# The raw weight blocks of block products go to Pool's DMA queue

## Chip, core and metric

The kernel runs on one core of a Trainium2 chip. The metric is device time in microseconds (us) for one execution; several executions are timed and their median is compared. The engines are named as the profile names them: PE (TensorE, matmuls), PEld (its weight loads), DVE (VectorE), ACT (ScalarE), POOL (GpSimd) and SP (SyncE, which here only issues DMAs). A name with q, such as SPq, is an engine's instruction queue.

## The reference, cut to what matters

The reference is one inference step of a two-layer decoder trunk for a prompt of 1024 tokens and 8 sample tokens that share all weights. What the change touches is the feed-forward block of each layer, with a model width of 1024 and a hidden width D_FF of 2816:

```python
def swiglu(h, w_gu, w_down):
    gate, up = jnp.split(h @ w_gu, 2, axis=-1)
    return (jax.nn.silu(gate) * up) @ w_down
```

Around it stand an HGRN2 recurrence or a stick-breaking attention, an attention into memory tokens, and RMS norms. All is float32.

## The kernel before, in words

Tokens are worked on in two groups, g = 0 (512 prompt tokens) and g = 1 (512 prompt tokens and the 8 sample tokens, 520 columns). Activations lie transposed, features on the 128 partitions. To keep float32 accuracy, every operand of a matmul is split into a high part (rounded to fp32r) and a low part (the rest), and each product is three matmuls: high by high, high by low, low by high. For a weight block this means a load of the raw float32 block, a cast on ACT (high part) and a subtraction on DVE (low part), then the matmuls. `split_w` (load at L254, cast L259, subtraction L260) does that for an ordinary block; its raw tile comes from the pool `wraw` with 5 buffers.

The hidden width is cut into 22 slices f of 128 columns, and these into five parts of 5, 5, 4, 4 and 4 slices (`PARTS`). A part computes gate and up for its slices and then adds their share of the down projection for all eight output blocks, with weights loaded by `split_w` (`w<-in_w_down` in the profile).

For most slices the gate and up products are ordinary. For group 1 some slices use **block products** instead: the two products (gate and up, each with two halves of the contracted width and two halves of the columns) are done as seven products of half size in place of eight, with sums of weight blocks and of activation blocks as operands. `ffn(1, 0, ...)`, layer 0, does so for slices 10 to 21; `ffn_w(1, ...)`, layer 1, for slices 4 to 21. That is 12 + 18 = 30 slices.

For each such slice `sums_here` loads four raw weight blocks a11, a21, a12, a22 of 128 x 512 floats (256 KB in 512 runs of 512 bytes) in the loop at L528, and hands back a function that makes the weight of product j. The sums are DVE additions at L535: product 1 needs a21 + a22 (in the profile `b<-w` or `b<-c`, the first addition of a slice), product 2 a11 + a21 + a22, product 5 a12 on top of that. Products 0, 3 and 6 take a11, a12 and a22 as they are. `gate_up_w` casts each weight on ACT (L560), subtracts on DVE (L561), runs 12 matmuls for each product (L570, 84 for a slice) and puts the seven results together on ACT and DVE (L577 to L594; the DVE steps L588 and L590 free PSUM banks into which later matmuls of the slice write).

Buffers: in layer 0 a slice's raw blocks take two tiles of the pool `cpool` (4 buffers, tile name `c`), in layer 1 two tiles of `apool` (8 buffers, four of them held by other data there; tile name `w`), and for slice 4 alone four tiles of `wraw`. So a slice's loads can start when the slice two before it has released its tiles: after the addition and the splits of a12, and after the split of a22 for product 6.

The order of the work is partly written out by hand (the `weave` and `drain` calls at the end) and otherwise set by the framework's planner: it lists the instructions of each engine and each DMA queue in an order found by a costed replay of the program, with the buffers of the pools given out in that replay. On the chip each engine and queue then runs its list strictly in order, and waits on semaphores. A different queue for a load therefore can change the listed order of other instructions too.

All direct DMAs stand in SP's queue. POOL's queue has only 32 gathers of cache pages (`page_loader`, L992, 256 KB each in 128 rows of 2 KB), which belong to the sample tokens of layer 1 and lie between the two stages with block products, apart from the first eight at the end of the first; besides, POOL builds constants in the first 14 us.

Of the kernel before, what the change touches and what calls it, by code (L numbers as in the profile page):

```python
# [23 lines left out]
def tile_decoder(  # L24
# [6 lines left out]
    nc = tc.nc  # L31
# [491 lines left out]
    def sums_here(l, f, raws, outs):  # L523
        a11, a12, a21, a22 = raws()
        for r, k0, m0 in (
            (a11, 0, f * P), (a21, 0, DFF + f * P), (a12, 512, f * P), (a22, 512, DFF + f * P),
        ):
            nc.sync.dma_start(  # L528
                r.rearrange("p (k m) -> p k m", m=P), w_gu[l][k0 : k0 + 512, m0 : m0 + P].rearrange("(k p) m -> p k m", p=P)
            )  # L530
        kept = {}

        def add(a, b):
            t = outs()
            nc.vector.tensor_add(t, a, b)  # L535
            return t

        def weight(j):
            if j == 1:
                return add(a21, a22)  # L540
            if j == 2:
                kept[3] = add(a11, a21)
                kept[2] = add(kept[3], a22)
                return kept[2]
            if j == 4:
                return kept[3]
            if j == 5:
                return add(kept[2], a12)
            return (a11, None, None, a12, None, None, a22)[j]

        return weight
# [51 lines left out]
    class ffn_w:  # L603
# [13 lines left out]
        def raws(self):  # L617
            if self.pi:
                ts = [apool.tile([P, 2, 512], F32, tag="a", name=nm("w")) for _ in range(2)]
                return [t[:, a, :] for t in ts for a in range(2)]  # L620
            return [wraw.tile([P, 512], F32, tag="w", name=nm("w")) for _ in range(4)]

        def part(self, pi):
# [4 lines left out]
            for j in range(nf):  # L628
                self.pi = pi
                if f0 + j < self.plain:  # L630
                    mt, ins = gate_up_q(l, f0 + j, self.x)
                    mids.append(mt)
                    with tc.issue_after(ins.ins):
                        for _ in range((1, 2, 1, 0)[j]):
                            next(self.sums, None)
                else:
                    mids.append(gate_up_w(
                        sums_here(l, f0 + j, self.raws, B),
                        self.ops, self.spl, lambda: [Q(i) for i in range(4)]
                    )[0])  # L640
                yield
# [33 lines left out]
    class ffn:  # L675
# [14 lines left out]
        def part(self, pi):  # L690
# [5 lines left out]
            for j in range(nf):  # L696
                if f0 + j >= self.prod:
                    mt, gate = gate_up_w(
                        sums_here(l, f0 + j, self.raws, B),
                        self.ops, lambda: wspl.tile([P, 2, 512], F32R, tag="ws", name=nm("ws")), self.quads,  # L700
                    )
                    mids.append(mt)
                    yield
                    continue
                pg = proj(g, w_gu[l], 0, ND, (f0 + j) * P, self.xt)
                sg = silu(None, pg, g)
                pu = proj(g, w_gu[l], 0, ND, DFF + (f0 + j) * P, self.xt)
                nc.vector.tensor_mul(sv(sg, g), sv(sg, g), pv(pu, g))  # L708
                mt = M(F32R)
                split_to((mt[:, 0, :n], mt[:, 1, :n]), sg[:, :n])  # L710
                mids.append(mt)
                yield
# [853 lines left out]
```

## Time and profile before

| What | us |
|---|---|
| median of 3 runs | 2492.56 (2491.49 to 2495.53) |
| the profiled execution, its own time | 2501.9 |
| its span, first to last instruction | 2500.2 |
| PE busy in the span | 2457.2 |
| DVE busy | 1669.7 |
| ACT busy | 1202.1 |
| POOL busy | 46.6 |
| packets of SP's DMA queue, as a share of 16 DMA engines | 38.1% |

The page gives busy times for each engine, forty slices of the span, the DMA queues, the chain of work that ended last, and groups of instructions by line with what ended the idle time before them. The longer views are: who waited for whom, the chain in order of time, the timeline of one stretch, and busy times by stretch. Matmuls are pipelined, so their durations overlap and a busy PE is not a PE at its peak. The stretch with block products of layer 0 runs from about 1237 to 1419 us of the span, that of layer 1 from about 2187 to 2460 us.

### The profile page before, as it was taken

The page shows a single profiled execution, that of the slowest core. Times are in us where ns is not written, and L with a number is a line of the kernel's source. Part 1 is how long each engine was busy: PE and PEld are TensorE (multiplying, and loading weights), DVE is VectorE, ACT ScalarE, POOL GpSimd, SP SyncE. Part 2 cuts the span into 40 slices and gives each one's busy share as a digit, 9 for nine tenths or more (in the row PEclk, how much of TensorE's full clock was granted, in tenths as well). Part 3 has the DMA queues.
Part 4 walks back from the last instruction along what each step waited for, and adds up shares of the span by engine and source line. Part 5 has one row for each costly group of instructions (what it writes and reads, how often), then busy time and mean ns, then how long its engine had stood idle before and what let it go on. Part 6 is the DMA issues. An engine that isn't in the chain of part 4 may idle for free.

```text
span 2500.2 us, 40342 instructions
## 1 busy us (share of the span) xinstructions
PE 2457.2 (98%) x15421; PEld 2156.9 (86%) x15421; DVE 1669.7 (67%) x2972; ACT 1202.1 (48%) x2315; POOL 46.6 (2%) x59
## 2 busy tenths in 40 slices
PE   8999999999999999999999999999999999999998
PEld 6888988877877898999999989877777798999997
DVE  5766556654766585655877785677677558676775
ACT  5446544243433454555544554555454445554444
POOL 1000000000000000000000100021000000000000
PEclk9999999999999999999999999999999999999999
DMA  5352252233643447422233445553444243343331
GB/s 185 113 164 71 72 156 81 60 110 116 179 124 99 127 133 224 127 87 68 75 100 94 147 136 188 158 162 113 135 144 118 77 127 118 110 128 101 95 92 48
DMA packets 451595, 297.88 MB, mean 119 GB/s; under 512 B 17605, under 2 KB 414482, under 8 KB 451402
## 3 DMA queue, kind: packets, MB, share of 16 engines
q1 hardware_dynamic: 448842, 286.92, 38.1%
q0 software_dynamic: 2560, 8.39, 1.1%
q8 instruction: 121, 1.98, 0.3%
q14 instruction: 72, 0.59, 0.1%
HBM read 265.44 MB, written 29.80 MB: 118 GB/s over the span
## 4 chain that ended last, share of the span: by engine, by line
PE 89%; DVE 5%; DMA 2%; ACT 2%; issue 1%; POOL 0%; SPq 0%; DVEq 0%; ACTq 0%
PE mm L273 58%; PE q L570 5%; PE q L654 5%; PE s L1188 2%; PE q L509 2%; PE mm L1056 2%; PE mm L570 2%; PE s L570 1%; PE s L911 1%; PE s L1344 1%; PE s L870 1%; DVE b L535 1%; PE mm L820 1%; PE ns L965 1%; PE mm L847 1%
## 5 line engine op out<-in xcount | busy, mean ns | idle before, releaser
L273 PE MATMUL mm<-x,ws 128*128 128x512 f32 (+1 forms) x6624 | 1193.7, 338 | 0.0
L273 PEld LDWEIGHTS mm<-x,ws 128*128 128x128 f32 x6624 | 1009.5, 188 | 152.3 <-issue 12.2
L259 ACT CAST ws<-w 128x512 fp32r<-128x512 f32 (+1 forms) x664 | 390.5, 589 | 669.3 <-PE mm L273 518.5
L260 DVE TENSOR_TENSOR ws<-w,ws 128x512 fp32r<-128x512 f32 (+1 forms) x664 | 429.0, 649 | 262.3 <-ACT ws L259 254.0
L273 PE MATMUL mm<-m,ws 128*128 128x512 f32 (+1 forms) x2112 | 395.0, 343 | 0.3
L273 PEld LDWEIGHTS mm<-m,ws 128*128 128x128 f32 x2112 | 324.6, 189 | 50.9 <-issue 3.2
L654 PE MATMUL q<-m,ws 128*128 128x260 f32 x1056 | 128.8, 283 | 0.0
L654 PEld LDWEIGHTS q<-m,ws 128*128 128x128 f32 x1056 | 127.2, 188 | 0.4 <-ACT hT L484 0.2
L570 PE MATMUL q<-y,ws 128*128 128x260 f32 x864 | 114.3, 285 | 7.2 <-DVE t L588 7.1
L570 PEld LDWEIGHTS q<-y,ws 128*128 128x128 f32 x864 | 107.7, 189 | 9.2 <-DVE t L588 9.2
L446 DVE TENSOR_TENSOR r<-r,mm 128x512 f32<-128x512 f32 (+1 forms) x96 | 66.0, 687 | 57.0 <-PE mm L273 56.4
L560 ACT CAST ws<-b 128x512 fp32r<-128x512 f32 x120 | 74.4, 621 | 57.3 <-PE q L654 15.7
L561 DVE TENSOR_TENSOR ws<-b,ws 128x512 fp32r<-128x512 f32 x120 | 82.4, 688 | 22.9 <-ACT ws L560 21.4
L290 DVE TENSOR_SCALAR t<-mm 128x512 f32<-128x512 f32 (+1 forms) x70 | 48.3, 690 | 61.7 <-PE mm L273 61.5
L570 PE MATMUL q<-x,ws 128*128 128x260 f32 x648 | 87.7, 285 | 0.0
L570 PEld LDWEIGHTS q<-x,ws 128*128 128x128 f32 x648 | 82.7, 191 | 0.0
L708 DVE TENSOR_TENSOR t<-t,mm 128x512 f32<-128x512 f32 (+1 forms) x54 | 37.2, 688 | 56.3 <-PE mm L273 56.0
L294 DVE TENSOR_TENSOR t<-t,t 128x512 f32<-128x512 f32 (+1 forms) x54 | 37.4, 692 | 54.0 <-ACT t L293 54.0
L313 DVE TENSOR_TENSOR st<-st,n 128x512 f32<-128x512 f32 (+1 forms) x98 | 67.0, 691 | 6.6 <-ACT n L312 5.0
L280 ACT CAST m<-t 128x512 fp32r<-128x512 f32 (+1 forms) x88 | 54.8, 623 | 17.0 <-DVE t L708 8.5
L281 DVE TENSOR_TENSOR m<-t,m 128x512 fp32r<-128x512 f32 (+1 forms) x88 | 60.8, 691 | 1.5 <-ACT m L280 0.7
L570 PE MATMUL mm<-a,ws 128*128 128x260 f32 x432 | 59.0, 285 | 1.7 <-DVE t L590 1.3
(362 smaller groups left out, 2974.3 us busy)
## 6 DMA issues: line engine op xcount, KB each, us to landing
w<-in_w_gu SPq DMA_DIRECT2D x304, 256.0 KB
w<-in_w_down SPq DMA_DIRECT2D x160, 256.0 KB
w<-in_w_in_a SPq DMA_DIRECT2D x80, 256.0 KB
w<-in_w_o SPq DMA_DIRECT2D x64, 256.0 KB
c<-in_w_gu SPq DMA_DIRECT2D x48, 256.0 KB
w<-in_w_mem_kv SPq DMA_DIRECT2D x32, 256.0 KB
c<-in_cache_mem_k SPq DMA_DIRECT2D x16, 512.0 KB
c<-in_cache_mem_v SPq DMA_DIRECT2D x16, 512.0 KB
```

What stands on the lines that cost most here:

```text
L259: nc.scalar.copy(ws[:, 0, :n, :], raw[:, :n, :])
L260: nc.vector.tensor_sub(ws[:, 1, :n, :], raw[:, :n, :], ws[:, 0, :n, :].bitcast(F32))
L273: nc.tensor.matmul(ps[:, a, : PW[g]], wt, xt[k][:, xi, o : o + PW[g]], start=(k == 0 and wi == 0), stop=(k == nk - 1 and wi == 2),)
L280: nc.scalar.copy(dst[0], src)
L281: nc.vector.tensor_sub(dst[1], src, dst[0].bitcast(F32))
L313: nc.vector.tensor_add(acc[:, :n], acc[:, :n], t[:, :n])
L446: nc.vector.tensor_add(dst, dst, pv(ps, g))
L509: nc.tensor.matmul(pp[a][:, :h], wt, xt[k][:, xi, a * h : (a + 1) * h], start=(k == 0 and wi == 0), stop=(k == ND - 1 and wi == 2),)
L560: nc.scalar.copy(w[:, 0, :], src)
L561: nc.vector.tensor_sub(w[:, 1, :], src, w[:, 0, :].bitcast(F32))
L570: nc.tensor.matmul(ps[:, :h], w[:, wj, k * P : (k + 1) * P], x[:, xi, :], start=(first and k == 0 and wi == 0), stop=(k == 3 and wi == 2), ...
L654: nc.tensor.matmul(pp[a][:, :h], wt, mids[k][:, xi, a * h : (a + 1) * h], start=(k == 0 and wi == 0), stop=(k == nf - 1 and wi == 2),)
```

## The change

The four loads of `sums_here` are issued from GpSimd's (Pool's) DMA queue. Everything else, the loads of `split_w` among it, stays on SP's queue. Per execution these are 30 x 4 = 120 loads of 256 KB.

```diff
@@ -525,7 +525,7 @@ def sums_here(l, f, raws, outs):
         for r, k0, m0 in (
             (a11, 0, f * P), (a21, 0, DFF + f * P), (a12, 512, f * P), (a22, 512, DFF + f * P),
         ):
-            nc.sync.dma_start(
+            nc.gpsimd.dma_start(
                 r.rearrange("p (k m) -> p k m", m=P), w_gu[l][k0 : k0 + 512, m0 : m0 + P].rearrange("(k p) m -> p k m", p=P)
             )
```

## The prediction

> **What bounds the kernel now.** First the page's busy times, then the waits by engine, then the two stretches with block products (1237 to 1419 us and 2187 to 2460 us).
>
> ```profile
> span 2500.2 us, 40342 instructions
> PE 2457.2 (98%) x15421; PEld 2156.9 (86%) x15421; DVE 1669.7 (67%) x2972; ACT 1202.1 (48%) x2315; POOL 46.6 (2%) x59
> ```
>
> PE is busy for 2457.2 of 2500.2 us, so a change of DMA queues can win little: 43 us in the whole kernel, most of it elsewhere. Busy times by stretch show what lies open where these loads are used (the first number after the stretch's length is PE's):
>
> ```profile
> 1225.00:1300.00 75.00, 72.15 (x561) 69.04 (x560) 60.53 (x114) 38.34 (x81) 0.00 (x0) 1.00 0.37 109
> 1300.00:1360.00 60.00, 58.34 (x471) 56.77 (x470) 43.47 (x75) 28.15 (x57) 0.00 (x0) 1.00 0.33 97
> 2200.00:2300.00 100.00, 96.59 (x790) 96.16 (x790) 72.95 (x137) 49.03 (x102) 0.00 (x0) 0.98 0.36 105
> 2300.00:2400.00 100.00, 96.83 (x795) 95.46 (x794) 75.29 (x138) 48.90 (x98) 0.00 (x0) 1.00 0.36 104
> ```
>
> PE's open time in these four is 2.85 + 1.66 + 3.41 + 3.17 = 11.1 us. Now the waits: of SP for the loads' buffers, of DVE for the loads, of PE for DVE (us in total, times, longest).
>
> ```profile
> SPq L528 <- DVE ws L561: 163.2, 31, 15.1
> SPq L528 <- DVE t L594: 66.4, 18, 6.5
> DVE b L535 <- DMA w<-in_w_gu: 19.0, 14, 3.6
> DVE b L535 <- DMA c<-in_w_gu: 3.5, 6, 1.5
> PE q L570 <- DVE t L588: 7.1, 6, 3.3
> PE mm L570 <- DVE t L590: 1.3, 1, 1.3
> PE mm L570 <- DVE t L588: 0.6, 1, 0.6
> ```
>
> Read downwards these are one mechanism. SP sits at L528 because DVE has not yet released the raw tiles (229.6 us), not because SP is busy. As soon as they are released the load starts, and for 20 slices DVE waits for its landing, 22.5 us in all. DVE runs in order, so L588 and L590 of the slice before stand behind the waiting addition, and PE loses 7.1 + 1.3 + 0.6 = 9.0 us in 8 places. One round of it, from the chain in order of time:
>
> ```profile
> 2226.16 0.69 DVE ws L561
> ...
> 2227.20 0.05 SPq L528
> 2227.25 0.05 issue
> 2227.30 3.46 DMA w<-in_w_gu
> ...
> 2230.85 0.69 DVE b L535
> ...
> 2235.28 0.35 DVE t L588
> 2235.62 0.04 issue
> 2235.67 21.96 PE q L570 x180
> ```
>
> The split at 2226.16 ends near 2226.85 and releases a tile; its two loads go out, the second at 2227.30, and both have landed at 2230.76. So release to second landing is 2230.76 - 2226.85 = **3.9 us** on SP's queue. DVE then has some 4.8 us of its own work up to L588, and PE waits for that. The timeline says how much of DVE's wait came through:
>
> ```profile
> 2224.51 0.42 DVE L588 TENSOR_TENSOR t<-t,q 128x260 f32<-128x260 f32 x1
> ...
> 2230.85 0.69 DVE L535 TENSOR_TENSOR b<-w 128x512 f32<-128x512 f32 x1 [0.85 <-DMA w<-in_w_gu]
> ...
> 2235.20 0.42 DVE L588 TENSOR_TENSOR t<-t,q 128x260 f32<-128x260 f32 x1
> ...
> 2235.67 1.50 PEld L570 LDWEIGHTS q<-y,ws 128*128 128x128 f32 x12 [0.33 <-DVE t L588]
> ```
>
> 0.85 us of waiting on DVE cost PE's weight load 0.33, so about 0.5 us was covered; the slice takes 2235.20 - 2224.51 = 10.7 us. The loads are just in time, and every further microsecond from release to landing meets a path with at most half a microsecond left.
>
> **The change part by part.**
>
> *Removed from SP: 120 issues.* The view of line L528 gives their lengths (ns, least, median, most):
>
> ```profile
> L528 SPq DMA_DIRECT2D w<-in_w_gu x72: 367/498/1947, 2130.4 to 2428.5; - x72
> L528 SPq DMA_DIRECT2D c<-in_w_gu x48: 367/502/1388, 992.0 to 1390.6; - x48
> ```
>
> That is 120 x 0.5 = 60 us of SP, and SP's 229.6 us of waiting at L528. What stood behind are loads of the down projection. I cost this at nothing: in the table of waits no PE wait in these stretches leads to `w<-in_w_down`, and what holds the loads of L528 themselves is DVE's release, which holds them on any queue. The bytes and DMA engines stay the same. If SP's freer queue loads ordinary blocks earlier, they find the `wraw` buffers as full as before.
>
> *Added to POOL: 120 issues.* The trace has no direct DMA on POOL; the nearest row is the gather L992, with the same 256 KB in 128 rows where these have 512.
>
> ```profile
> L992 POOL DMA_INDIRECT c<-in_cache_sb_k,pidx x16: 940/946/1288, 1397.8 to 1646.6; - x16
> DMA to landing us min/median/max: 3.2/3.5/5.8
> 1407.22 0.94 POOL L992 DMA_INDIRECT c<-in_cache_sb_k,pidx  x1 [4.10 <-DVE ws L561]
> 1408.47 0.95 POOL L992 DMA_INDIRECT c<-in_cache_sb_k,pidx  x1 [0.30 <-issue]
> 1690.74 2.88 POOL L992 DMA_INDIRECT c<-in_cache_sb_v,pidx  x1 [10.24 <-DVE c L964]
> 1693.92 3.01 POOL L992 DMA_INDIRECT c<-in_cache_sb_v,pidx  x1 [0.30 <-issue]
> ```
>
> A gather holds POOL for 0.95 us, the next begins 1.25 us after it (SP: 0.42), and it lands 3.5 us after its start. The second of two loads so lands 1.25 + 3.5 = 4.75 us after release, against 3.9 now: **0.85 us later**. Four loads hold POOL for 4 x 1.25 = 5.0 of a slice's 10.7 us, so the queue keeps up. Bounds: below, nothing is added (a direct load carries no index to fetch, and half a microsecond is covered); above, four times the rows at four times 0.95 = 3.8 us each, second landing 3.8 + 0.3 + 3.8 + (3.5 - 0.95) = 10.5 us, 6.6 later. Between ends so far apart I take 1.0 us, by the row of equal bytes, with a little for the rows; a generation of 1.3 us makes it 0.3 + 2 x 1.3 + 2.55 - 3.9 = 1.6, which I keep for the range.
>
> One page states a smaller step: the Trainium skill, "DMA: Bandwidth & Descriptors", section "Latency and other measured facts", gives a first byte after about 0.6 us for SP's path and about 1 us for Pool's. By that 0.4 us the sum below would be 8 x 0.4 = 3.2 us; no run here shows a direct load from POOL yet.
>
> *The wait that moves.* The release wait now stands in POOL's queue. Behind it wait only later raw loads and the first eight gathers, which already waited for the same tiles (at 1397.8, after L594). Their next neighbour is issued at 1608, so a delay of some us is covered by 200.
>
> *DVE, ACT, PE.* No instruction is added or removed. The first additions (L535) wait 1.0 us longer where they are just in time. Of the 20 waiting slices, the 8 that already reach PE have no cover: 8 x 1.0 = **8.0 us**. The 12 others still have part of the half microsecond, and the planner may list the additions later on DVE, so I take nothing for them; without that, 12 x 1.0 come on top.
>
> **Sum.** On the profiled execution 2501.9 (span 2500.2 and 1.7 around it) + 8.0 = 2509.9 us. That execution lies 9.3 us over the median of the timed runs, 2492.6; the same 8.0 on the median gives **2500.6 us**.
>
> **Rivals.**
>
> *Faster: the planner moves the addition behind L588 and L590.* The place is DVE's list around each L535. The planner replays a load on Pool's queue at another length; if it then lists the first addition of a slice two or three DVE instructions later, DVE's wait no longer stands before the step that PE needs. It decides when the addition is listed after L590: L588 at 2235.20 comes 4.35 us after the addition, L590 at 2236.14, so a shift of the pair by the added microsecond is not enough by itself, but the additions feed matmuls several us later and have room. Price: the 9.0 us of PE's waits, 2492.6 - 9.0 = 2483.6; with all open time of the four stretches 2492.6 - 11.1 = 2481.5. For it: DVE is idle a quarter of these stretches (72.95 and 75.29 of 100). Against: latency grows, and the trace does not show the planner's costs. Chance 0.28.
>
> *No change: absorbed.* The added delay and the shifted list cancel, since PE has 0.5 us of cover in most slices and only 8 of 30 lost anything: within 5 us of 2492.6. Chance 0.22. Here also falls the case that the change does nothing because DVE's release, not the queue, sets the start.
>
> *Much slower: generation on POOL is the bound.* The gathers at 1690.74 and 1693.92 took 2.88 and 3.01 us in a stretch where DVE was packed with additions and products. Four loads at 3.2 us apart are 12.8 us, over the 10.7 of a slice: 2.1 us for 20 to 30 slices, 42 to 63 us, so 2535 to 2556. Against: at 1407 to 1409, inside a stretch of block products, a gather took 0.94 and 0.95. Chance 0.08.
>
> A rule bears on that rival. The Trainium skill, "SBUF — State Buffer", section "Who interferes with whom", says that VectorE's two-port modes lock GpSimd out of writing descriptors, and that `tensor_tensor` has no such mode but contends with GpSimd's reads. A gather reads its indices, so by that rule 3 us would be the gather's and not a direct load's. The DVE rows of the block products quoted here are TENSOR_TENSOR, and the trace has both 0.95 and 3.01 us among such.
>
> **How the numbers follow.** Forecast (slower by the longer way to landing, +5 to +32): 0.42. Much slower: 0.08. Absorbed: 0.22. Faster: 0.28. About 0.2%, 5 us, is what a measurement of this kernel can tell from no change. So slower 0.50, same 0.22, faster 0.28. The predicted time is 2500.6. The range goes down to 2481.5, the end of the faster rival, and up to 2492.6 + 20 x 1.6 = 2524.6, where all 20 waiting slices pay the longer step; it leaves out the much slower case and tails, under 0.2. As cases of both signs hold much of the chance, the forecast's own range is 2497.6 to 2524.6.
>
> **What would show it.** Right: POOL rows at L528 of about 1 to 1.3 us; release to second landing near 4.8 to 5.5 us; DVE's wait at L535 for `in_w_gu` above 22.5 us; PE's waits for L588 and L590 above 9.0 us. Wrong: L535 listed behind L590, with PE's wait gone (faster); POOL rows of 3 us and POOL busy for most of a slice (much slower); or PE losing time outside the two stretches, which would be the planner's new order and not the queue.

## The result and the profile after

The changed kernel takes **2522.36 us** (median of 6 runs, 2519.61 to 2524.32); the kernel before took 2496.35 beside it (6 runs, 2491.49 to 2500.96). The ratio is 1.0105, with a 95% interval of 1.0089 to 1.012: slower by 26 us, between 22 and 30. The profiled execution after took 2519.61, the lowest of its six, and the one before 2501.9, so the two traces differ by only 17.7 of the 26 us. Three of those six executions before are the ones of the table ahead of the change; in 63 other executions, run beside the experiments and not beside the changed kernel, the same kernel had medians of 2498.19 to 2500.91, and against those the changed one is 21 to 24 us slower. The cost may therefore lie near the lower end of the interval.

The page, with PE's and POOL's busy time:

```profile
span 2517.9 us, 40396 instructions
PE 2459.7 (98%) x15421; PEld 2159.0 (86%) x15421; DVE 1670.3 (66%) x2972; ACT 1202.4 (48%) x2315; POOL 137.9 (5%) x179
```

PE, DVE and ACT have the same number of instructions and nearly the same busy time; POOL has 120 more. So the time went mostly into waiting. The table of waits after (us in total, times, longest):

```profile
PE q L570 <- DVE t L588: 14.1, 12, 3.5
PE mm L570 <- DVE t L590: 8.4, 8, 2.1
PE mm L570 <- DVE t L588: 0.6, 1, 0.6
DVE b L535 <- DMA w<-in_w_gu: 28.9, 15, 3.8
DVE b L535 <- DMA c<-in_w_gu: 12.1, 11, 2.3
```

DVE's waits for the raw blocks grew from 22.5 us in 20 places to 41.0 in 26, PE's waits for L588 and L590 from 9.0 us in 8 places to 23.1 in 21. These are the rows the prediction named. Busy times of the two stretches with block products say that most of it lies there; first the kernel before, then the changed one, each over its own stretches (the first number after the length is PE's):

```profile
1237.00:1420.00 183.00, 178.49 (x1430) 173.42 (x1429) 134.77 (x235) 92.03 (x186) 7.86 (x8) 1.00 0.38 116
2187.00:2460.00 273.00, 265.82 (x2182) 263.79 (x2181) 194.06 (x360) 132.86 (x272) 0.00 (x0) 0.99 0.34 99
```

```profile
1240.00:1430.00 190.00, 178.92 (x1421) 173.87 (x1422) 132.94 (x231) 91.01 (x180) 40.10 (x50) 0.99 0.36 111
2200.00:2480.00 280.00, 265.94 (x2180) 263.44 (x2179) 194.35 (x361) 131.95 (x270) 47.74 (x65) 0.99 0.32 95
```

Nearly the same PE work takes 7 us longer in each; PE's open time (length less busy time) went from 4.5 + 7.2 to 11.1 + 14.1 us, 13.5 more. Over the whole span it grew from 43.0 to 58.2, by 15.2 us, and PE's busy time by 2.5; together these are the 17.7.

The clock granted to PE (the last column but two) shows no difference over 0.01 here, but it has a small share. Inside the block products the fourteen traces of this study show PE at half clock for 3.41 us at a time, or twice that, and each time this begins within 5 us of the start of a PE wait of at least 1.8 us. In the kernel before it happens once, after a wait of 3.3 us at 2210.3; in the changed one twice, after 2.1 us at 1357.8 and 3.5 us at 2220.6. Not every such wait is followed by it: one of 2.3 us, in the last kernel told here, was not. Over whole executions the mean granted clock was 0.9947 in the six runs after and 0.9961 to 0.9967 in those of before beside the experiments. Among the 63 other executions of before, the six granted 0.995 average 2502.6 us and the 29 granted 0.997 average 2497.4, 2.6 us for each thousandth; by that, as an estimate, the difference of about 0.0017 is worth some 4 of the 26 us. If the wait is what brings the half clock on, as their order in time suggests, a long wait costs more than its own length.

Next the new issues on POOL, by the view of line L528:

```profile
L528 POOL DMA_DIRECT2D w<-in_w_gu x72: 747/747/793, 2141.0 to 2446.6; - x72
L528 POOL DMA_DIRECT2D c<-in_w_gu x48: 747/747/967, 974.2 to 1401.2; - x48
DMA to landing us min/median/max: 3.2/3.5/7.4
```

An issue is 0.75 us, near the gather's 0.95 and far from the bound of 3.8.

**Where the added time acts.** What the prediction read as a wait with some cover is a closed loop. DVE's timeline of the kernel before shows one turn (other rows left out):

```profile
2305.83 0.68 DVE L561 TENSOR_TENSOR ws<-w,ws 128x512 fp32r<-128x512 f32 x1
...
2310.57 0.69 DVE L535 TENSOR_TENSOR b<-w 128x512 f32<-128x512 f32 x1 [0.73 <-DMA w<-in_w_gu]
...
2316.20 0.68 DVE L561 TENSOR_TENSOR ws<-w,ws 128x512 fp32r<-128x512 f32 x1
```

The split that ends at 2306.51 releases a raw tile; the pair that is loaded into it has landed when the addition starts at 2310.57, **4.06 us** after release. From that addition DVE works through its list without a gap to the split that ends at 2316.88 and releases the next tile, **6.31 us** later. (The sums are listed one slice ahead: the split belongs to the slice before that of the addition, and the tile it releases takes blocks of the slice after.) One turn is 10.37 us, and a slice's 84 matmuls alone take PE 10.1 to 10.3 (in the slices without a wait). The loop already ran at PE's pace. The same turn after the change, then POOL's and PE's timelines of that time:

```profile
2319.56 0.68 DVE L561 TENSOR_TENSOR ws<-w,ws 128x512 fp32r<-128x512 f32 x1
...
2325.16 0.69 DVE L535 TENSOR_TENSOR b<-w 128x512 f32<-128x512 f32 x1 [1.58 <-DMA w<-in_w_gu]
...
2329.51 0.42 DVE L588 TENSOR_TENSOR t<-t,q 128x260 f32<-128x260 f32 x1
...
2330.79 0.68 DVE L561 TENSOR_TENSOR ws<-w,ws 128x512 fp32r<-128x512 f32 x1
```

```profile
2320.65 1.49 POOL L528 DMA_DIRECT2D w<-in_w_gu  x2 [2.32 <-DVE t L594]
```

```profile
2329.98 1.72 PE L570 MATMUL q<-y,ws 128*128 128x260 f32 x12 [0.84 <-DVE t L588]
```

The release at 2320.24 is followed by the first issue 0.41 us later (the row names L594, which ends just before; L561 is the split that released the tile). The pair takes 1.49 us on POOL, and the addition starts at 2325.16: 4.92 us after release. Then come the same 6.31 us to 2331.47. One turn is now **11.23 us**, 0.9 over PE's own, and L588, carried along behind the addition, reaches PE 0.84 late. Over 47 pairs before and 48 after, release to second landing has a median of 3.91 and 4.76 us: 0.85 later.

### The profile page after: what moved, and what is told of

Its sections match the earlier page's. It is cut to its first block, busy times and chain, and to the rows that moved or that the text cites. A ratio compares the mean times of both kernels' runs of the same rounds, so it can differ in the third digit from the quotient of the medians.

```text
span 2517.9 us, 40396 instructions
## 1 busy us (share of the span) xinstructions
PE 2459.7 (98%) x15421; PEld 2159.0 (86%) x15421; DVE 1670.3 (66%) x2972; ACT 1202.4 (48%) x2315; POOL 137.9 (5%) x179
## 5 line engine op out<-in xcount | busy, mean ns | idle before, releaser
L570 PE MATMUL q<-y,ws 128*128 128x260 f32 x864 | 114.5, 285 | 14.1 <-DVE t L588 14.1
L528 POOL DMA_DIRECT2D c<-in_w_gu x48 | 35.9, 753 | 1352.5 <-ACT ws L259 960.7
L561 DVE TENSOR_TENSOR ws<-b,ws 128x512 fp32r<-128x512 f32 x120 | 82.4, 688 | 22.1 <-ACT ws L560 21.8
L528 POOL DMA_DIRECT2D w<-in_w_gu x72 | 53.7, 750 | 648.3 <-DMA w<-in_w_gu 395.6
```

The source lines that it names most:

```text
L528: nc.gpsimd.dma_start(r.rearrange("p (k m) -> p k m", m=P), w_gu[l][k0 : k0 + 512, m0 : m0 + P].rearrange("(k p) m -> p k m", p=P))
L561: nc.vector.tensor_sub(w[:, 1, :], src, w[:, 0, :].bitcast(F32))
L570: nc.tensor.matmul(ps[:, :h], w[:, wj, k * P : (k + 1) * P], x[:, xi, :], start=(first and k == 0 and wi == 0), stop=(k == 3 and wi == 2), ...
```

## The experiments

All but the first differ from the kernel before by the lines shown. The median of before was 2500.91 beside the first four told here, 2499.31 beside those with half-size loads, with one load on SP and with product 3 first, and 2498.19 beside the others. Microseconds slower or faster are the ratio times that median.

**The kernel before, once more**, to see what a comparison can tell.

> The kernel before, unchanged, as a second profile and a null comparison. All theories: same time as before within 0.2%. Its profile shows how far PE's waits for L588 and L590 in the block products (9.0 us in the first profile) vary from one execution to another; expected 5 to 10 us.

2500.56 us, ratio 1.0002 (0.9992 to 1.0012). PE's waits for L588 and L590 come to 9.4 us here, against 9.0 in the first profile, so they hardly vary from one execution to another.

**By layer.** Only one layer's loads go to POOL:

```diff
-            nc.sync.dma_start(
+            (nc.gpsimd if l == 0 else nc.sync).dma_start(   # second run: l == 1
```

> Only the 48 loads of layer 0 (tile c) go to Pool's queue. The listed order of PE, DVE and ACT is the same as before, to the last instruction. Latency theory (the longer way from release to second landing, 4.7 in place of 3.9 us, meets DVE's in-order list and passes to PE): about +9 to +12 us, with PE's waits for L590 near 8 us as in the changed kernel. Rival, the planner's new order costs the time: 0, within 2 us. Rival, contention of POOL's generation with DVE: DVE instructions in 1237 to 1419 us grow by over 2%, which they did not in the changed kernel.

> Only the 72 loads of layer 1 (tile w) go to Pool's queue. Latency theory: the rest of the 26 us, about +8 to +16, so that the two halves add up to the whole. Rival, the planner's new order of DVE in layer 1: here the whole 26 us or most of it, since only layer 1 has a different DVE order.

Layer 0: 2509.47 us, ratio 1.0047 (1.0032 to 1.0061), 11.8 us slower. Layer 1: 2511.64, ratio 1.0045 (1.0031 to 1.006), 11.3 slower. Together 23 (each with an interval of 8 to 15), about the whole. In the first of the two kernels PE, DVE and ACT have the very instruction order of before, and it pays as much; so in layer 0 the planner's order isn't the cause. (In layer 1, DVE's list differs from before in 31 of 2972 places, and these runs don't part that from the landing.) DVE's busy time is 1670.5 us against 1669.7 before, so its instructions didn't grow either. The waits of the first kernel, of which L590's are layer 0's:

```profile
PE mm L570 <- DVE t L590: 9.3, 9, 2.6
PE q L570 <- DVE t L588: 6.5, 6, 3.6
```

**The second load of each pair only** (a12 and a22 on POOL, a11 and a21 on SP):

```diff
+            (nc.gpsimd if r is a22 or r is a12 else nc.sync).dma_start(
```

> The second load of each pair (a12 after a11, a22 after a21) goes to Pool's queue, the first stays on SP's, so both can start on the release without waiting for one another. Latency theory: the landing of the pair is that of the one POOL load, 0.40 to start and 3.3 to land = 3.7 us after release, against 3.9 before: 0 us, within 5. Rival, any load on POOL costs by itself (planner or contention): about half of 26, +10 to +15 us.

2507.8 us, ratio 1.0031 (1.0019 to 1.0044): 7.8 slower, between the two expectations. Release to second landing has a median of 4.16 us here, 0.25 over before, since the two queues start side by side; so three tenths of the delay, and of the time. The match is looser than it looks: in layer 1 the turns are about as before, and the loss lies in layer 0 and around the first slices of layer 1.

**Each pair by itself.** a21 and a22 are read by the first addition, a11 and a12 are released about 3 us earlier:

```diff
+            (nc.gpsimd if r is a21 or r is a22 else nc.sync).dma_start(   # second run: a11 or a12
```

> Only a21 and a22, the blocks of the first addition of a slice, go to Pool's queue; a11 and a12 stay on SP's. Theory (the loads of a21 and a22 land just in time, and the addition that waits for them stands on DVE ahead of L588 and L590): these two carry nearly all of the cost, 20 to 27 us over before, with PE's waits for L588 and L590 near 20 us and DVE's waits at L535 near 40. Rival (every load on Pool's queue costs alike, 120 loads for 26 us): half of it, about 13 us.

> The other half: only a11 and a12 go to Pool's queue. They are released some 3 us ahead of a21 and a22 in the traces, so by the theory 0.86 us more of landing is covered: within 4 us of before, PE's waits for L588 and L590 near 9 us. Rival (every load on Pool's queue costs alike): about 13 us over before.

With a21 and a22 on POOL: **2524.32 us, ratio 1.0107 (1.009 to 1.0123), 26.7 slower**. With a11 and a12: **2500.45, ratio 1.0008 (0.9998 to 1.0018)**. Both as the theory had it: half of the loads carry the whole cost, and 60 loads on POOL's queue cost nothing that can be measured. The waits of the first kernel, then those of the second:

```profile
PE q L570 <- DVE t L588: 15.3, 11, 4.2
PE mm L570 <- DVE t L590: 9.1, 9, 2.2
DVE b L535 <- DMA w<-in_w_gu: 32.6, 14, 7.6
DVE b L535 <- DMA c<-in_w_gu: 13.1, 11, 2.4
```

```profile
PE q L570 <- DVE t L588: 5.9, 6, 2.8
PE mm L570 <- DVE t L590: 1.5, 2, 0.9
DVE b L535 <- DMA w<-in_w_gu: 21.2, 14, 6.4
DVE b L535 <- DMA c<-in_w_gu: 4.0, 7, 1.3
```

The first table is like that of the changed kernel, the second like that of before. A cost of POOL's issue, of its queue or of the bytes as such is excluded by this pair of runs; what counts is when the two blocks of the first addition land.

**More and fewer loads on SP's queue**, to change the landing without POOL. First each block as two loads of 128 KB:

```diff
-            nc.sync.dma_start(
-                r.rearrange("p (k m) -> p k m", m=P), w_gu[l][k0 : k0 + 512, m0 : m0 + P].rearrange("(k p) m -> p k m", p=P)
+            for o in (0, 256): nc.sync.dma_start(
+                r[:, o : o + 256].rearrange("p (k m) -> p k m", m=P), w_gu[l][k0 + o : k0 + o + 256, m0 : m0 + P].rearrange("(k p) m -> p k m", p=P)
```

> All loads on SP's queue, as before, but each raw block in two loads of 128 KB, so a pair is four issues. Nothing is on POOL. Latency theory: the last of the four is issued 3 x 0.42 = 1.25 us after the first instead of 0.42, the pair lands about 4.7 us after release as on POOL's queue, and the time rises by about as much as with POOL, +20 to +28 us (28 us for each microsecond, from 7.7 us at 0.3 and 26 us at 0.85). Rival, POOL's use itself costs the time: about 0. If the smaller transfers land earlier than I think (4.3), +11.

2498.41 us, ratio 0.9995 (0.9986 to 1.0004): no change, a miss for the theory as I had it. Release to last landing is 4.1 us in the median, hardly later, because a load of half the size lands sooner after its issue (2.5 us in the median, against 3.35). And the planner listed DVE otherwise, as its timeline shows:

```profile
2300.51 0.68 DVE L535 TENSOR_TENSOR b<-w 128x512 f32<-128x512 f32 x1
...
2305.61 0.69 DVE L561 TENSOR_TENSOR ws<-w,ws 128x512 fp32r<-128x512 f32 x1
...
2310.67 0.68 DVE L535 TENSOR_TENSOR b<-w 128x512 f32<-128x512 f32 x1
```

From the addition to the end of the split are now 5.79 us in place of 6.31, so the loop has half a microsecond of room: the addition at 2310.67 waits for nothing, and the turn is 10.16 us, PE's own. The run therefore doesn't test the price of a later landing; it shows that DVE's listed order is the other half of the loop.

Then one load of 512 KB for each pair (slice 4 of layer 1 excepted, whose blocks lie in four tiles), on SP's queue and on POOL's (`ts[0]` is the tile that holds a11 and a12, `ts[1]` that of a21 and a22):

```diff
-            (a11, 0, f * P), (a21, 0, DFF + f * P), (a12, 512, f * P), (a22, 512, DFF + f * P),
+            (ts[0].rearrange("p a n -> p (a n)"), 0, D, f * P), (ts[1].rearrange("p a n -> p (a n)"), 0, D, DFF + f * P),
...
-            nc.sync.dma_start(
+            nc.sync.dma_start(     # second run: nc.gpsimd
```

> All loads on SP's queue, and both blocks of a pair (they lie in one tile) in one load of 512 KB, except for slice 4 of layer 1. Latency theory: the second issue's 0.42 us goes, the landing is bound by the transfer, so 3.6 to 3.8 us after release in place of 3.9: -3 to -9 us. If the 512 KB land in more than 4.0 us the time rises instead at 28 us per microsecond.

> Pool's queue, but one load of 512 KB for each pair, as in the run with one load on SP's queue (which was 5 us faster than before, with 3.96 us from release to landing). The spacing of 0.74 us between two loads is gone, the 0.40 us from release to the first issue stays. Theory (the landing decides): release to landing 4.3 to 4.5 us, so about half of the 0.86 us, and a time of before plus 5 to 11 us, 10 to 16 over the one load on SP. Rival (Pool's queue costs as such, by its issue or its gaps on the DMA engines): as the changed kernel less the 5 us, so about 20 us over before. Rival (only the number of issues counts): as before or a little faster.

On SP: **2493.58 us, ratio 0.998 (0.9971 to 0.9989), 5 us under before**, the one kernel of the study that beats both. Release to landing is 3.96 us, as before, and the turn no shorter than can be told; DVE's waits at L535 fell to 18.2 us and PE's for L588 and L590 to 5.9. What makes those waits shorter isn't settled.

On POOL: 2523.98, ratio 1.0102 (1.0085 to 1.0119), 25.5 slower, where 5 to 11 were expected; the rival's 20 came nearer, though a cost of POOL's queue as such had no trace in the run with a11 and a12. The size in the expectation was wrong: the view of DMA issues (KB of each, median us from issue to landing) has, first for SP's kernel and then for POOL's,

```profile
w<-in_w_gu SPq DMA_DIRECT2D x34, 512.0 KB, 3.8
```

```profile
w<-in_w_gu POOLq DMA_DIRECT2D x34, 512.0 KB, 4.6
```

The same load from POOL's queue lands 0.8 us later after its issue, and with the 0.40 us ahead of it release to landing is 5.12, not 4.3 to 4.5. DVE's timeline shows the loop with that latency:

```profile
2332.08 0.69 DVE L535 TENSOR_TENSOR b<-w 128x512 f32<-128x512 f32 x1 [1.70 <-DMA w<-in_w_gu]
...
2337.70 0.68 DVE L561 TENSOR_TENSOR ws<-w,ws 128x512 fp32r<-128x512 f32 x1
...
2343.56 0.69 DVE L535 TENSOR_TENSOR b<-w 128x512 f32<-128x512 f32 x1 [1.84 <-DMA w<-in_w_gu]
```

6.30 us of list and 5.18 from release to the next addition are a turn of 11.48. The delay over before is 1.2 us where the changed kernel has 0.85, and yet the time is the same; so the time isn't strictly proportional to the delay. A small part of this is the clock, of which the runs here were granted 0.9955 in the mean and those of the changed kernel 0.9947, worth some 2 us by the estimate above; the rest is open.

**a21 and a22 first.** As the single load on SP, with the two loads of a slice in the other order:

```diff
+            (ts[1].rearrange("p a n -> p (a n)"), 0, D, DFF + f * P), (ts[0].rearrange("p a n -> p (a n)"), 0, D, f * P),
```

> SP's queue, one load of 512 KB for each pair, and the pair a21, a22 loaded ahead of a11, a12, so that it takes the tile that is released 3 us earlier. Theory (the first addition of a slice waits for a21 and a22, and L588 stands behind it): DVE's waits at L535 fall from 18 us to under 8, PE's waits for L588 and L590 from 6 to under 3, and the time is 6 to 12 us under before. Rival (a11 and a12 are needed as early, by the second addition, which follows at once): the wait only moves to the second addition, time as with one load in the old order, about 5 us under before, or slower.

2500.06 us, ratio 1.0003 (0.9993 to 1.0013): the rival was right. DVE's timeline shows the wait at the second addition, which reads a11:

```profile
2308.83 0.69 DVE L535 TENSOR_TENSOR b<-w,w 128x512 f32<-128x512 f32 x1 [0.64 <-DMA w<-in_w_gu]
...
2316.03 0.69 DVE L535 TENSOR_TENSOR b<-w 128x512 f32<-128x512 f32 x1 [0.23 <-DMA w<-in_w_gu]
2319.25 0.69 DVE L535 TENSOR_TENSOR b<-w,w 128x512 f32<-128x512 f32 x1 [0.72 <-DMA w<-in_w_gu]
```

Whichever pair comes second is waited for, since the additions stand close together. DVE's waits at L535 are 37.9 us here, against 18.2 with the same loads in the old order.

**Product 3 ahead of products 1 and 2**, to give the additions one product more of cover, with the loads on SP and on POOL:

```diff
-        product(pd, 1, True)
-        product(pb, 2)
-        nc.scalar.activation(pc[:, :h], pb[:, :h], AF.Copy, scale=-1.0)
         product(pa, 3)
         sg = T()
         nc.scalar.activation(sg[:, :h], pa[:, :h], AF.Silu)
+        product(pd, 1, True)
+        product(pb, 2)
+        nc.scalar.activation(pc[:, :h], pb[:, :h], AF.Copy, scale=-1.0)
```

> Loads on SP's queue; in gate_up_w product 3 (block a12, from the earlier pair) and its silu are listed ahead of products 1 and 2, so that the first addition is needed one product (12 matmuls, 1.44 us) later. Latency theory: the just-in-time wait gets some 1.4 us of cover, PE's waits for L588 and L590 fall from 9 to 0 to 3 us: -4 to -9 us. The planner's list is new here, so an unrelated shift of either sign within 5 us may lie on top.

> The same order of products with the four loads on POOL's queue; the lists of PE, DVE and ACT differ from the SP version in a few places only. Latency theory: the 0.85 us of longer latency fit into the 1.4 us of cover, so it is within 8 us of the SP version, in place of 26 without the new order. Rival, contention or POOL's use itself: again about 26 us above the SP version.

On SP 2506.57, ratio 1.0031 (1.0022 to 1.0041), 7.7 slower; on POOL 2526.65, ratio 1.0112 (1.0096 to 1.0127), 28 slower and 20 over the SP version. Both missed, for different reasons. On SP, PE's waits for L588 and L590 did fall, from 9.0 to 3.8 us, near the 0 to 3 expected. But PE's busy time is 2466.1 us, 8.9 more: its slices take about 10.5 us each, also where no addition waits for a load, in place of 10.1 to 10.3. That is a cost of the new order itself, some 0.3 x 30 = 9 us by estimate; what in it lengthens the slices isn't shown. On POOL, DVE's list from the addition to the release is 6.2 us, which with 4.8 to 4.9 from release to addition makes turns of 11.1, over PE's 10.5. There the cover was put on PE, and the loop runs through DVE.

**The runs side by side.** For layer 1, from DVE's timelines: median from release to the first addition, from addition to next release, and three turns inside a part (the 3rd and 4th of the first part, the 1st of the second).

| kernel | release to addition | addition to release | turns | us over before |
|---|---|---|---|---|
| before | 4.0 | 6.3 | 10.1, 10.4, 10.4 | 0 |
| a11, a12 on POOL | 4.0 | 6.3 | 10.3, 10.6, 10.4 | 2.0 |
| one load, SP | 3.9 | 6.3 | 10.3, 10.2, 10.2 | -5.0 |
| changed | 4.8 | 6.3 | 11.0, 11.3, 11.2 | 26.2 |
| a21, a22 on POOL | 4.8 | 6.3 | 11.1, 11.2, 11.1 | 26.7 |
| second load of a pair on POOL | 4.2 | 6.3 | 10.2, 10.6, 10.4 | 7.8 |
| half-size loads, SP | 4.3 | 5.8 | 10.1, 10.1, 10.1 | -1.2 |
| one load, POOL | 5.2 | 6.3 | 11.2, 11.6, 11.4 | 25.5 |
| product 3 first, SP | 3.9 | 6.7 | 10.3, 10.7, 10.6 | 7.7 |
| product 3 first, POOL | 4.9 | 6.2 | 11.1, 11.3, 11.1 | 28.0 |

The kernels with turns of 11 us pay 25 to 28, those at 10.1 to 10.4 next to nothing, and the half-size loads, later but in a shorter list, don't pay either. Two rows don't fit by this stretch and its loop: the second loads on POOL lose their 7.8 us elsewhere, and product 3 first on SP loses its 7.7 in PE's longer slices, as told above. The table is of layer 1 alone, but layer 0 has the same loop. In the kernel before, two of its first additions start at 1327.37 and 1337.96 us, a turn of 10.59 (6.58 from addition to release, 4.01 from release to the next addition); in the changed one at 1334.18 and 1345.58, a turn of 11.40 (6.60 and 4.80).

## Why the prediction was right in its sign and short in its size

*What bounds the kernel: right.* Release, load, waiting addition, and L588 and L590 behind it on DVE: this chain carried the change, and the two runs on single pairs show it.

*SP relieved: right.* Nothing was won or lost by it; 60 loads taken off SP's queue made no difference (a11 and a12 alone).

*Landing 0.85 us later: right, from another make-up.* The sum was 1.25 of spacing + 3.5 of landing = 4.75 from release; measured are 0.40 to the first issue + 0.74 of spacing + 3.5 of landing = 4.64 by the single medians, and 4.76 as the median of the pairs. The gather's row gave the right sum by luck: the issue is shorter than I took it (0.74 against 1.25 of spacing), and the start that I had at zero takes 0.40, which nearly makes up for it.

*The page's 0.4 us.* By the first-byte figures of the Trainium skill, "DMA: Bandwidth & Descriptors", section "Latency and other measured facts", the step would have been 0.4 us and the time, as an estimate, 3.2 more; the trace shows 0.85 for a pair, and the time rose by 26. The rows don't show the first byte: the 0.40 us seen here lies between release and issue.

*"The 12 others still have part of the half microsecond, and the planner may list the additions later on DVE, so I take nothing for them": this step failed.* The sum was 8 waiting slices x 1.0 = 8.0 us; measured are 26, with waits in 26 places on DVE and 21 on PE. The half microsecond isn't there anew in every slice. The addition that waits delays the split that releases the next tile, so the lateness is handed on, and the cover is spent once in a part of four or five slices: in layer 1, additions that waited 0.85, 0.51 and 0.78 us in three slices on end (2230.85 to 2251.40 us) before, wait 1.66, 1.33 and 1.13 after. In the loop each turn pays what it is longer than PE's slice: 11.2 - 10.3 = 0.9 us. For the 26 additions that wait this is an estimate of 26 x 0.9 = 23 us, against 22 to 30 measured; it leaves the clock out. The clue was in the rows quoted for the prediction: release to landing 3.9 and a slice of 10.7; the missing row was that from the addition to the next release, 6.31, which makes the two a sum of 10.2.

*The wait that moved: right.* Nothing that waits behind it on POOL reached PE.

*The faster rival* (additions listed later) falls: DVE's list changed a little in layer 1 alone, and layer 0, with no instruction moved, paid as much. Its kind of effect is real: the kernel with half-size loads got it from the planner by chance. *Absorbed* falls: the cover was not there for every slice. *Much slower* falls: an issue took 0.747 us in the median and 0.967 at most, and never 3, with DVE's additions and splits beside it. By the rule of the Trainium skill, "SBUF — State Buffer", section "Who interferes with whom", long issues among `tensor_tensor` would be the gather's own; the trace agrees as far as it goes: the gathers of `in_cache_sb_v` reach 3.01 us after as before, at a median of 1.05, and no direct load comes near that. But those gathers run in another stretch than the direct loads, so the rule isn't tested by them.

The predicted 2500.6 lies 22 us under the result; the range's end, 2524.6, held it only by luck: a delay taken too long (1.6) met a number of slices taken too small (20).

Open stays: why a landing later by 1.2 us costs no more than one by 0.85; why one load instead of two gains 5 us on SP; how much of layer 1's cost its changed DVE list has; and whether another tile of raw blocks, or additions listed later on DVE, would take the load out of the loop, which wasn't tried.

## What to carry to other kernels

Where a load waits for a buffer and an instruction waits for the load, follow the chain on until it comes back to the release: if it closes, its turn is the load's latency plus the list from the waiting instruction to the next release, and this sum is to be held against the other engine's time for one round. At par, added latency is paid again in round after round, whatever cover a single wait seems to have. Of several loads, move those whose data are not waited for: here half of them went to the slower queue for nothing.

## What the runs showed of the hardware

- A direct load of 256 KB in 512 rows of 512 bytes held POOL for 0.747 us, shorter than a gather of 256 KB in 128 rows (0.94 at the least); a load of 512 KB held it for 0.884. Twice the rows so added 18%, and the number of rows was not the main part of the time.
- On POOL's queue the first of two loads started 0.40 us after the release (SP: 0.03), the second 0.74 us later (SP: 0.41).
- After its issue a load of 256 KB landed in 3.5 us from POOL's queue and in 3.35 from SP's in these stretches; one of 512 KB in 4.7 against 3.9 in the median, in both layers alike. (The view of DMA issues gives 4.4 for layer 0's on SP, a median of only the three loads that it could follow.) The larger load has the wider gap between the queues; the cause wasn't looked into.
- Inside the block products every stretch of half clock on PE (3.41 us, or twice that) came within 5 us of the start of a PE wait of 1.8 to 4.4 us, in all the traces that show one.
